# Shift and scale sums accumulated in PSUM, a third of the weight remainders made by GpSimd, and a flatter rate of requests for the first units

## Chip, cores and metric

The kernel runs on one core of a Trainium2 chip. The metric is the device time of one execution in microseconds, median of several runs. PE is TensorE, DVE is VectorE, ACT is ScalarE, POOL is GpSimd, and SP is the engine whose queue issues the DMAs.

## What is computed

One decoder layer for 256 tokens of width 4096, all in float32 (cut to what matters here):

```
mod = silu(c) @ w_ada + b_ada              # c: one vector of 4096; w_ada: 4096 x 12288
shift, scale, gate = split(mod, 3)
h = rmsnorm(x) * norm_gain
h = h * (1 + scale) + shift
proj = h @ w_in                            # 4096 x 12288
q, k, v, g_attn, u_pool, g_pool = split(proj)
y_attn = longnet_mixture(q, k, v) * silu(g_attn)       # 16 heads of 128
y_pool = multiscale_pool(u_pool, w_pool) * silu(g_pool)
y = concat(y_attn, y_pool) @ w_out         # 4096 x 4096
out = rmsnorm(x + gate * y) * final_gain
```

The weights are read once from HBM, 485 MB, and used for 256 tokens only.

## The kernel before

**Products.** A float32 weight tile is split into two parts that PE can multiply fast: ScalarE casts it (`wh`, line 237), and VectorE subtracts the cast from the original (`wl`, the remainder, line 238). The tokens are split in the same way (`hh`, `hl`). A *piece* is 2 rows of 128 of `w_in` by 512 columns, one tile `raw` of 512 KB; it makes 12 products of 128x512 (line 248): 8 that need `wh`, then 4 that need `wl`. There are 7 buffers for `raw`, and 3 each for `wh` and `wl`.

**Units.** h needs shift and scale, and these are sums over the whole of `w_ada`. The 4096 rows of h are therefore built in 16 *units* of 256 rows. For a unit 16 *tasks* are asked for (`ada_tasks`), each a `raw` tile of 512 KB of `w_ada`, on which VectorE does two steps of sum += weight * scalar (line 161, the first step of a unit line 159) into `aacc`, 128x512, in SBUF. `build_h` then has PE sum `aacc` over the partitions (line 208, four products with one column), VectorE makes the factors (lines 211 to 213), ScalarE makes h (line 221) and its cast `hh` (223), VectorE the remainder `hl` (224).

**Which work runs when.** The 24 chunks of 512 columns of `w_in` are visited in turn, as long as units are built. A *visit* (line 276) multiplies the units that are ready and that this chunk has not had yet, in one or more pieces, into one of two PSUM tiles `mm`. A chunk's first visit is copied to SBUF by ScalarE (line 289), every later one is added there by VectorE (line 291). After each piece of n rows the planner (`ada_hook`) gains n * RATES[units built] of credit, and asks for a task, at 1.456 each, while credit is above zero. A unit counts as ready two pieces after it is built. So RATES sets how soon units come, how many pieces a visit has, and how much VectorE and the DMA engines do per piece. After the 16 units the chunks get their remaining pieces, attention and pooling run in between, and the last product follows; the change does not touch that part.

Each engine runs its own queue in order. The order in it is not that of the code: the framework under the kernel lays the instructions out by its own estimate of times. PSUM has 8 banks; `mm` takes two times two, and a pool of four (`misc()`, named `psm`) serves all the rest.

Of the kernel before, what the change touches and what calls it, by code (L numbers as in the profile page):

```python
# [7 lines left out]
F32 = mybir.dt.float32  # L8
F32R = mybir.dt.float32r
AF = mybir.ActivationFunctionType  # L10
ALU = mybir.AluOpType
AX = mybir.AxisListType

P = 128
# [15 lines left out]
HB = 2  # L30
A0 = 1
WIN = 5
LAG = 2
RATES = (0.8, 0.8, 0.8, 0.5, 0.46, 0.5, 0.5, 0.5, 0.48, 0.5, 0.5, 0.54)
DEPTH = 3
HOLD = 1
EARLY = 4
# [10 lines left out]
PSB = 2  # L48
PSMB = 4
LINE = 512  # L50
RAW = PIECE * CH
ADA_COST = 0.728 * PIECE

# [2 lines left out]
def tile_hybrid_block(  # L56
# [17 lines left out]
    nc = tc.nc  # L74
# [6 lines left out]
    def slot_a(shape, dtype=F32):  # L81
        return accp.tile(shape, dtype, name="sa", bufs=16, align_bytes=LINE)

    def slot_b(shape, dtype=F32):
        return accp.tile(shape, dtype, name="sb", bufs=8, align_bytes=LINE)

# [3 lines left out]
    def misc():  # L90
        return ps_m.tile([P, CH], F32, name="psm")

    def raw_tile():
        return strm.tile([P, RAW], F32, name="raw", bufs=RAWB)

# [21 lines left out]
    adap = ada_cm.enter_context(tc.tile_pool(name="ada", bufs=2, side="right"))  # L117
# [37 lines left out]
    def ada_acc(acc, rt, kts, width, init=None):  # L155
        for i, kt in enumerate(kts):
            r = rt[:, i * width:(i + 1) * width]
            if kt == 0 and init is None:
                nc.vector.tensor_scalar(out=acc, in0=r, scalar1=cact[:, 0:1], scalar2=None, op0=ALU.mult)
            else:  # L160
                nc.vector.scalar_tensor_tensor(out=acc, in0=r, scalar=cact[:, kt:kt + 1],  # L161
                                               in1=init if kt == 0 else acc,
                                               op0=ALU.mult, op1=ALU.add)
# [3 lines left out]
    def late_work(f, lag=None):  # L167
        delayed.append(f)
        while len(delayed) > (HOLD if lag is None else lag):
            delayed.pop(0)()  # L170

    def flush_work():
        while delayed:
            delayed.pop(0)()

    def ada_tasks(u, pool):
        w = 2 * UNITS[u] * P
        n = RAW // w
        cs = slice(US[u] * P, US[u + 1] * P)
        acc = []  # L180
        tasks = []
        for a in range(0, KT, n):
            kts = list(range(a, min(KT, a + n)))

            def f(kts=kts):
                if not acc:
                    acc.append(pool.tile([P, 2 * HB * P], F32, name="aacc")[:, 0:w])
                rt = raw_tile()
                m = len(kts)
                v = rt[:, 0:m * w].rearrange("p (n s d) -> p n s d", n=m, s=2)  # L190
                if m == 1:
                    nc.sync.dma_start(out=v[:, 0], in_=wa_v[:, kts[0], 0:2, cs])
                else:
                    for i in range(2):
                        nc.sync.dma_start(out=v[:, :, i], in_=wa_v[:, kts[0]:kts[-1] + 1, i, cs])
                late_work(lambda: ada_acc(acc[0], rt, kts, w))
            tasks.append(f)
        return acc, tasks
# [4 lines left out]
    def build_h(u, acc, pool, xT):  # L203
        flush_work()
        uk, k0 = UNITS[u], US[u]
        pc = misc()
        for j in range(2 * uk):
            nc.tensor.matmul(pc[:, j:j + 1], lhsT=acc[:, j * P:(j + 1) * P], rhs=ones, start=True, stop=True)  # L208
        s12 = const.tile([P, 2, HB], F32, name="s12", bufs=2)
        ks = slice(k0, k0 + uk)  # L210
        nc.vector.tensor_tensor(out=s12[:, 0, 0:uk], in0=pc[:, 0:uk], in1=colB[:, ks], op=ALU.add)
        nc.vector.tensor_tensor(out=s12[:, 1, 0:uk], in0=pc[:, uk:2 * uk], in1=gainc[:, ks], op=ALU.mult)
        nc.vector.tensor_tensor(out=s12[:, 1, 0:uk], in0=s12[:, 1, 0:uk], in1=gb[:, ks], op=ALU.add)  # L213
        for a in range(0, uk, 2):
            kk = k0 + a
            if kk % HB == 0:
                htile[kk // HB] = [pool.tile([P, HB, S], F32R, name=n, align_bytes=LINE) for n in ("hh", "hl")]
            hh, hl = [v[:, kk % HB:kk % HB + 2] for v in htile[kk // HB]]
            hf = strm.tile([P, 2, S], F32, name="hf")
            for i in range(2):  # L220
                nc.scalar.activation(out=hf[:, i], in_=xT[:, kk + i], func=AF.Identity,  # L221
                                     scale=s12[:, 1, a + i:a + i + 1], bias=s12[:, 0, a + i:a + i + 1])
            nc.scalar.copy(out=hh, in_=hf)
            nc.vector.tensor_tensor(out=hl, in0=hf, in1=hh.bitcast(F32), op=ALU.subtract)
            for i in range(2):
                hs[kk + i] = (hh[:, i], hl[:, i])

    def split_piece(src, n, spare=False):
        rt = raw_tile()
        v = rt.rearrange("p (k n) -> p k n", n=CH)  # L230
        nc.sync.dma_start(out=v[:, 0:n], in_=src)
        if spare:
            wh, wl = [slot_a([P, PIECE, CH], F32R) for _ in range(2)]
        else:
            wh = strm.tile([P, PIECE, CH], F32R, name="wh", bufs=WHB, align_bytes=LINE)
            wl = strm.tile([P, PIECE, CH], F32R, name="wl", bufs=WLB, align_bytes=LINE)
        nc.scalar.copy(out=wh[:, 0:n], in_=v[:, 0:n])  # L237
        nc.vector.tensor_tensor(out=wl[:, 0:n], in0=v[:, 0:n], in1=wh[:, 0:n].bitcast(F32), op=ALU.subtract)  # L238
        return wh, wl

    def products(pt, hv, wh, wl, first, last):
# [102 lines left out]
    for u in range(A0):  # L344
        build_h(u, first[u][0][0], hp, xT)
# [5 lines left out]
    def ada_hook(n):  # L351
        st = state
        st["credit"] += n * RATES[min(st["built"], len(RATES) - 1)]
        st["age"] += 1
        while st["cur"] and st["cur"][1] and st["credit"] > 0:
            if len(st["cur"][1]) == 1 and min(used) < ((US[st["built"] + 1] - 1) // HB - WIN + 1) * HB:
                st["credit"] = 0.0
                break
            st["cur"][1].pop(0)()
            st["credit"] -= ADA_COST  # L360
        if st["cur"] and not st["cur"][1]:
            u = st["built"]
            build_h(u, st["cur"][0][0], hp, xT)
            st["built"] += 1
            st["age"] = 0
            st["cur"] = ada_tasks(u + 1, adap) if u + 1 < NU else None
        if st["age"] >= LAG:
            st["ready"] = st["built"]
# [3 lines left out]
    while state["ready"] < NU:  # L372
# [7 lines left out]
        else:  # L380
            ada_hook(1.0)
    hooks.remove(ada_hook)

    x_cm.close()
    ada_cm.close()
# [3 lines left out]
    def wide_tile(dtype):  # L389
        return late.tile([P, HG, S], dtype, name="tq", bufs=3, align_bytes=LINE)  # L390

# [345 lines left out]
```

## Time and profile before

| | |
|---|---|
| time, median of 3 runs | 1567.88 us (1565.35 to 1568.74) |
| the profiled execution: time, span | 1567.34 us, 1565.4 us |
| PE busy | 1516.3 us (97%), 7043 products |
| VectorE busy | 1405.4 us (90%) |
| ScalarE busy | 697.6 us (45%) |
| GpSimd busy | 0.7 us |
| chain that ended last, by engine | PE 91%, VectorE 3%, DMA 3% |
| read from HBM | 485.55 MB |

The profile is of one execution. Its views give busy time in stretches, the instructions in order of time with what ended the idle time before each, and groups of equal instructions. PE's weight loads (PEld) run beside its products and are the place where a wait of PE shows. Products are pipelined, so their own lengths overlap.

### The profile page before, as it was taken

How to read it: one execution, taken by the hardware profiler on the slowest of the kernel's cores; microseconds unless marked ns; L12 is line 12 of the kernel's file. 1: busy time of each engine (PE TensorE's matmuls, PEld its weight loads, DVE VectorE, ACT ScalarE, POOL GpSimd, SP SyncE). 2: the span in 40 equal slices, each digit the busy share in tenths (PEclk: the TensorE clock that was granted, in tenths of full speed). 3: DMA queues.
4: the chain of work that ended last, by engine and by line, in shares of the span. 5: the costliest groups of instructions: out<-in, count | busy, mean ns of one | idle time of the engine just before them, and what ended most of it. 6: DMA issues, size and time to landing. Idle time of an engine off the chain costs nothing.

```text
span 1565.4 us, 20360 instructions
## 1 busy us (share of the span) xinstructions
PE 1516.3 (97%) x7043; PEld 1257.5 (80%) x7043; DVE 1405.4 (90%) x1759; ACT 697.6 (45%) x820; POOL 0.7 (0%) x5
## 2 busy tenths in 40 slices
PE   2999999999999999999999999999999999999997
PEld 2877888888888888888888888888898888888775
DVE  5988999999999998899999998989988788898886
ACT  4655344443443434344344344556554443444433
POOL 0000000000000000000000000000000000000000
PEclk9999999999999999999999999999999999999999
DMA  9999999999999999899999998867778899998886
GB/s 331 363 335 362 321 331 321 324 308 336 327 310 327 312 330 313 294 326 326 354 340 331 330 333 307 290 226 242 231 250 273 287 357 347 318 339 324 320 305 250
DMA packets 324087, 491.11 MB, mean 314 GB/s; under 512 B 19320, under 2 KB 150664, under 8 KB 323984
## 3 DMA queue, kind: packets, MB, share of 16 engines
q1 hardware_dynamic: 323984, 489.82, 92.2%
q8 instruction: 55, 0.90, 0.2%
q14 instruction: 48, 0.39, 0.1%
HBM read 485.55 MB, written 4.19 MB: 313 GB/s over the span
## 4 chain that ended last, share of the span: by engine, by line
PE 91%; DVE 3%; DMA 3%; issue 1%; ACT 1%; SPq 0%; DVEq 0%; ACTq 0%
PE mm L248 83%; DVE aacc L161 1%; PE psm L614 1%; PE psm L248 1%; DMA raw<-in_w_ada_dram 1%; DMA raw<-in_w_in_dram 1%; PE psm L208 1%; DVE wl L238 1%; ACT wh L237 1%; PE psm L523 0%; PE psm L524 0%; PE psm L522 0%; DMA sb<-in_x_dram 0%; DMA raw<-in_w_out_dram 0%; PE psm L565 0%
## 5 line engine op out<-in xcount | busy, mean ns | idle before, releaser
L237 ACT CAST wh<-raw 128x1024 fp32r<-128x1024 f32 x514 | 538.5, 1050 | 700.0 <-PE mm L248 497.9
L238 DVE TENSOR_TENSOR wl<-raw,wh 128x1024 fp32r<-128x1024 f32 x514 | 624.5, 1218 | 45.1 <-ACT wh L237 41.9
L248 PE MATMUL mm<-wh,hh 128*128 128x512 f32 x1536 | 605.4, 394 | 4.8 <-ACT wh L237 3.8
L248 PE MATMUL mm<-wh,hl 128*128 128x512 f32 x1536 | 599.6, 390 | 0.0
L248 PE MATMUL mm<-wl,hh 128*128 128x512 f32 x1536 | 414.2, 391 | 0.6 <-DVE wl L238 0.6
L161 DVE SCALAR_TENSOR_TENSOR aacc<-raw,cact,aacc 128x512 f32<-128x512 f32 x496 | 371.0, 748 | 31.4 <-DMA raw<-in_w_ada_dram 23.8
L248 PEld LDWEIGHTS mm<-wh,hh 128*128 128x128 f32 x1536 | 288.8, 188 | 67.0 <-ACT wh L237 7.2
L248 PEld LDWEIGHTS mm<-wl,hh 128*128 128x128 f32 x1536 | 288.4, 188 | 61.1 <-DVE wl L238 1.4
L248 PEld LDWEIGHTS mm<-wh,hl 128*128 128x128 f32 x1536 | 288.9, 188 | 58.3 <-issue 0.2
L248 PE MATMUL mm<-wh,sa 128*128 128x512 f32 x896 | 224.0, 392 | 1.9 <-ACT wh L237 1.9
L248 PEld LDWEIGHTS mm<-wh,sa 128*128 128x128 f32 x896 | 167.7, 188 | 39.7 <-ACT wh L237 3.4
L161 DVE SCALAR_TENSOR_TENSOR gacc<-raw,cact,gacc 128x512 f32<-128x512 f32 x248 | 185.5, 748 | 13.5 <-DMA raw<-in_w_ada_dram 9.8
L248 PE MATMUL mm<-wl,sa 128*128 128x512 f32 x448 | 119.8, 389 | 0.0
L291 DVE TENSOR_TENSOR sa<-mm,sa 128x1024 f32<-128x1024 f32 x92 | 112.1, 1218 | 8.5 <-PE mm L248 8.4
L248 PEld LDWEIGHTS mm<-wl,sa 128*128 128x128 f32 x448 | 84.0, 188 | 17.5
L291 DVE TENSOR_TENSOR sb<-mm,sb 128x1024 f32<-128x1024 f32 x48 | 58.5, 1219 | 7.3 <-PE mm L248 7.3
L328 PE MATMUL psm<-diag_r,sb 128*128 128x128 f32 x128 | 16.9, 300 | 15.9 <-DVE diag_r L320 15.9
L221 ACT ACTIVATE hf<-xT,s 128x256 f32<-128x256 f32 x32 | 17.5, 595 | 27.9 <-DVE s L213 27.9
L328 PEld LDWEIGHTS psm<-diag_r,sb 128*128 128x128 f32 x128 | 16.6, 215 | 16.1 <-DVE diag_r L320 16.1
L289 ACT COPY sa<-mm 128x1024 f32<-128x1024 f32 x16 | 16.3, 1016 | 14.2 <-PE mm L248 14.1
L248 PE MATMUL psm<-wh,sa 128*128 128x512 f32 x80 | 20.1, 394 | 1.4 <-ACT wh L237 1.4
L248 PEld LDWEIGHTS psm<-wh,sa 128*128 128x128 f32 x80 | 14.8, 188 | 5.3 <-ACT wh L237 2.2
(113 smaller groups left out, 618.1 us busy)
## 6 DMA issues: line engine op xcount, KB each, us to landing
raw<-in_w_in_dram SPq DMA_DIRECT2D x384, 512.0 KB, 5.7
raw<-in_w_ada_dram SPq DMA_DIRECT2D x512, 256.0 KB, 5.3
raw<-in_w_ada_dram SPq DMA_DIRECT2D x128, 512.0 KB, 6.5
raw<-in_w_out_dram SPq DMA_DIRECT2D x128, 512.0 KB, 6.8
sb<-in_x_dram SPq DMA_DIRECT2D x16, 512.0 KB, 6.4
raw<-in_w_pool_dram SPq DMA_DIRECT2D x8, 512.0 KB, 4.7
out_dram<-sb SPq DMA_DIRECT2D x16, 256.0 KB, 2.6
fg<-in_final_gain_dram SPq DMA_DIRECT2D x8, 256.0 KB, 4.7
```

Of the source, the lines that this page charges most:

```text
L161: nc.vector.scalar_tensor_tensor(out=acc, in0=r, scalar=cact[:, kt:kt + 1], in1=init if kt == 0 else acc, op0=ALU.mult, op1=ALU.add)
L208: nc.tensor.matmul(pc[:, j:j + 1], lhsT=acc[:, j * P:(j + 1) * P], rhs=ones, start=True, stop=True)
L221: nc.scalar.activation(out=hf[:, i], in_=xT[:, kk + i], func=AF.Identity, scale=s12[:, 1, a + i:a + i + 1], bias=s12[:, 0, a + i:a + i + 1])
L237: nc.scalar.copy(out=wh[:, 0:n], in_=v[:, 0:n])
L238: nc.vector.tensor_tensor(out=wl[:, 0:n], in0=v[:, 0:n], in1=wh[:, 0:n].bitcast(F32), op=ALU.subtract)
L248: nc.tensor.matmul(pt[t], lhsT=hv[i][p][:, t * P:(t + 1) * P], rhs=w[:, i], start=started, stop=ended)
L289: nc.scalar.copy(out=accs[ch], in_=pt)
L291: nc.vector.tensor_tensor(out=accs[ch], in0=pt, in1=accs[ch], op=ALU.add)
L328: nc.tensor.matmul(px[:, i * S + t * P:i * S + (t + 1) * P], lhsT=xs[q][:, t, (2 * a + i) * P:(2 * a + i + 1) * P], rhs=diag_r[:, t], star ...
L614: nc.tensor.matmul(pt[t], lhsT=h[:, t * P:(t + 1) * P], rhs=w, start=False, stop=last and e == len(seq) - 1)
```

## The change

The sums of a unit grow in a bank of PSUM out of the pool of four instead of `aacc`; as PE can't read PSUM, ScalarE copies the finished 128x512 sums to SBUF (`aflat`) before the four products. While units are built, every third remainder is made by GpSimd. And RATES changes: 0.62 for the first five units in place of 0.8, 0.8, 0.5 and 0.46 (the entry in front counts for none). The diff:

```diff
-RATES = (0.8, 0.8, 0.8, 0.5, 0.46, 0.5, 0.5, 0.5, 0.48, 0.5, 0.5, 0.54)
+RATES = (0.62, 0.62, 0.62, 0.62, 0.62, 0.5, 0.5, 0.5, 0.48, 0.5, 0.5, 0.54)
+SHARE = (1, 3)
...
                 if not acc:
-                    acc.append(pool.tile([P, 2 * HB * P], F32, name="aacc")[:, 0:w])
+                    acc.append(misc()[:, 0:w])
...
     def build_h(u, acc, pool, xT):
         flush_work()
         uk, k0 = UNITS[u], US[u]
+        flat = adap.tile([P, 2 * HB * P], F32, name="aflat")
+        nc.scalar.copy(out=flat[:, 0:2 * uk * P], in_=acc)
+        acc = flat
         pc = misc()
...
+    share = {"on": True, "n": 0}
+
     def split_piece(src, n, spare=False):
...
-        nc.vector.tensor_tensor(out=wl[:, 0:n], in0=v[:, 0:n], in1=wh[:, 0:n].bitcast(F32), op=ALU.subtract)
+        eng = nc.gpsimd if share["on"] and share["n"] % SHARE[1] >= SHARE[1] - SHARE[0] else nc.vector
+        share["n"] += 1
+        eng.tensor_tensor(out=wl[:, 0:n], in0=v[:, 0:n], in1=wh[:, 0:n].bitcast(F32), op=ALU.subtract)
...
     hooks.remove(ada_hook)
+    share["on"] = False
```

The change also moves instructions in the queues. Line numbers of the new kernel are up to 8 higher (238 is 246, 291 is 299), and the number behind a name tells one buffer's use from the next.

VectorE before, where the second round of visits has begun: mm_1255 and mm_1298 are the visits that end with pieces 36 and 38, and wl_1302, wl_1325 and wl_1350 the remainders of pieces 37, 38 and 39.

```order
L238 TENSOR_TENSOR wl_1302<-raw_1299,wh_1301 128x1024
L291 TENSOR_TENSOR sa_410<-mm_1255,sa_410 128x1024
L161 SCALAR_TENSOR_TENSOR aacc_1157<-raw_1317,cact_74,aacc_1157 128x512
L238 TENSOR_TENSOR wl_1325<-raw_1322,wh_1324 128x1024
L161 SCALAR_TENSOR_TENSOR aacc_1157<-raw_1317,cact_74,aacc_1157 128x512
L161 SCALAR_TENSOR_TENSOR aacc_1157<-raw_1340,cact_74,aacc_1157 128x512 x2
L291 TENSOR_TENSOR sb_436<-mm_1298,sb_436 128x1024
L238 TENSOR_TENSOR wl_1350<-raw_1347,wh_1349 128x1024
```

In the first add here PE's next remainder (wl_1302) is already ahead of the add; at the last one it (wl_1350) stands behind.

VectorE now, at the start of the second round, which has visits of one piece: mm_1072, mm_1097 and mm_1122 are pieces 29, 30 and 31; wl_1076, wl_1126 and wl_1151 are the remainders of 29, 31 and 32. That of 30 is GpSimd's.

```order
L246 TENSOR_TENSOR wl_1076<-raw_1073,wh_1075 128x1024
L162 SCALAR_TENSOR_TENSOR psm_854<-raw_1091,cact_74,psm_854 128x512 x2
L299 TENSOR_TENSOR sa_381<-mm_1072,sa_381 128x1024
L162 SCALAR_TENSOR_TENSOR psm_854<-raw_1116,cact_74,psm_854 128x512 x2
L299 TENSOR_TENSOR sa_407<-mm_1097,sa_407 128x1024
L246 TENSOR_TENSOR wl_1126<-raw_1123,wh_1125 128x1024
L162 SCALAR_TENSOR_TENSOR psm_854<-raw_1141,cact_74,psm_854 128x512 x2
L299 TENSOR_TENSOR sb_433<-mm_1122,sb_433 128x1024
L246 TENSOR_TENSOR wl_1151<-raw_1148,wh_1150 128x1024
```

The remainders of pieces 31 and 32 stand behind the adds of pieces 30 and 31.

ScalarE before, at the first unit (xT is x transposed, hf is h before its split):

```order
L332 COPY xT<-psm 128x512 x12
L237 CAST wh<-raw 128x1024
L221 ACTIVATE hf<-xT,s_321 128x256 x2
L332 COPY xT<-psm 128x512
L223 CAST hh<-hf 128x512
```

There h comes right behind the first cast. ScalarE now, at the same place:

```order
L340 COPY xT<-psm 128x512 x12
L243 CAST wh<-raw 128x1024
L208 COPY aflat<-psm 128x512
L340 COPY xT<-psm 128x512
L225 ACTIVATE hf<-xT,s_323 128x256 x2
L340 COPY xT<-psm 128x512
L227 CAST hh<-hf 128x512
```

The new copy stands between the cast and h, and one copy of xT has moved ahead of h.

## Rows read from the trace of the kernel before

**Rows 1.** Windows: length; busy PE, PEld, DVE, ACT, POOL; PEclk, DMA share, GB/s

```profile
47.30:166.70 119.40, 114.93 (x498) 92.04 (x497) 107.24 (x129) 69.23 (x74) 0.00 (x0) 0.99 1.03 348
107.60:138.70 31.10, 30.06 (x131) 22.82 (x129) 27.59 (x37) 16.66 (x18) 0.00 (x0) 1.00 1.07 368
166.70:640.00 473.30, 473.30 (x2117) 393.01 (x2116) 446.13 (x507) 191.32 (x193) 0.00 (x0) 1.00 0.97 322
```

**Rows 2.** Timeline 937 to 941: start, length, engine, line, operation, [idle before <-releaser]

```profile
937.43 1.05 ACT L237 CAST wh<-raw 128x1024 fp32r<-128x1024 f32 x1 [1.67 <-PE mm L248]
...
937.93 1.53 DVE L161 SCALAR_TENSOR_TENSOR aacc<-raw,cact,aacc 128x512 f32<-128x512 f32 x2
...
939.38 1.22 DVE L238 TENSOR_TENSOR wl<-raw,wh 128x1024 fp32r<-128x1024 f32 x1
...
940.15 1.05 ACT L237 CAST wh<-raw 128x1024 fp32r<-128x1024 f32 x1 [1.67 <-PE mm L248]
```

**Rows 3.** Timeline of PE's weight loads: those that begin after idle time

```profile
79.58 0.19 PEld L248 LDWEIGHTS mm<-wh,hh 128*128 128x128 f32 x1 [2.47 <-ACT wh L237]
...
111.00 0.19 PEld L248 LDWEIGHTS mm<-wh,hh 128*128 128x128 f32 x1 [0.74 <-ACT wh L237]
...
131.22 0.19 PEld L248 LDWEIGHTS mm<-wh,hh 128*128 128x128 f32 x1 [0.41 <-ACT wh L237]
138.65 0.19 PEld L248 LDWEIGHTS mm<-wh,hh 128*128 128x128 f32 x1 [1.15 <-ACT wh L237]
163.16 0.76 PEld L248 LDWEIGHTS mm<-wl,hh 128*128 128x128 f32 x4 [1.06 <-DVE wl L238]
...
662.26 0.19 PEld L248 LDWEIGHTS mm<-wh,hh 128*128 128x128 f32 x1 [1.35 <-issue]
```

**Rows 4.** Windows, the ten microseconds after the first stop

```profile
80.00:90.00 10.00, 10.00 (x42) 8.11 (x40) 7.39 (x9) 4.77 (x6) 0.00 (x0) 0.83 1.07 363
```

**Rows 5.** Timeline of VectorE, 160 to 164 us

```profile
160.75 1.22 DVE L291 TENSOR_TENSOR sb<-mm,sb 128x1024 f32<-128x1024 f32 x1 [0.19 <-PE mm L248]
161.89 2.35 DVE L238 TENSOR_TENSOR wl<-raw,wh 128x1024 fp32r<-128x1024 f32 x2
```

**Rows 6.** Timeline of ScalarE, 77 to 81 us

```profile
77.58 1.01 ACT L289 COPY sb<-mm 128x1024 f32<-128x1024 f32 x1 [1.70 <-PE mm L248]
78.48 2.08 ACT L237 CAST wh<-raw 128x1024 fp32r<-128x1024 f32 x2
```

**Rows 7.** Groups of VectorE: out<-in, shapes, count | busy us, mean ns

```profile
L161 DVE SCALAR_TENSOR_TENSOR aacc<-raw,cact,aacc 128x512 f32<-128x512 f32 x496 | 371.0, 748 | 31.4 <-DMA raw<-in_w_ada_dram 23.8
...
L527 DVE SCALAR_TENSOR_TENSOR y<-psm,colA,tq 128x256 f32<-128x256 f32 x16 | 7.0, 477 | 2.1 <-PE psm L524 2.1
```

**Rows 8.** Instructions of lines 332 and 542: ns min/median/max, first and last start

```profile
L332 ACT COPY xT<-psm x16: 565/586/590, 30.7 to 47.6; 128x512 f32<-128x512 f32 x16
...
L542 POOL MEMSET bz<- x1: 526/526/526, 958.1 to 958.1; 128x512 f32 x1
```

**Rows 9.** Timeline of all engines, 28 to 48 us

```profile
28.61 14.13 DVE L161 SCALAR_TENSOR_TENSOR aacc<-raw,cact,aacc 128x512 f32<-128x512 f32 x18
...
42.16 1.05 ACT L237 CAST wh<-raw 128x1024 fp32r<-128x1024 f32 x1
...
42.89 1.02 PE L208 MATMUL psm<-ones,aacc 128*128 128x1 f32 x8 [1.25 <-DVE aacc L161]
...
43.77 3.82 PE L328 MATMUL psm<-diag_r,sb 128*128 128x128 f32 x32
...
44.47 1.09 ACT L221 ACTIVATE hf<-xT,s 128x256 f32<-128x256 f32 x2 [1.26 <-DVE s L213]
...
45.93 0.62 ACT L223 CAST hh<-hf 128x512 fp32r<-128x512 f32 x1
...
46.61 0.68 DVE L224 TENSOR_TENSOR hl<-hf,hh 128x512 fp32r<-128x512 f32 x1
...
47.66 0.39 PE L248 MATMUL mm<-wh,hl 128*128 128x512 f32 x1
```

## The prediction, made before the changed kernel ran

> **What bounds the kernel now.** First, where TensorE stands still. [rows 1] cuts the building of the units into stretches; the first column after the name is PE's busy time. From 166.7 us on PE is busy 473.30 of 473.30 us: whatever is made shorter on another engine there gains nothing. Before it, from 47.3 to 166.7, PE is busy 114.93 of 119.40.
>
> Next, what a piece takes. In [rows 2] ScalarE's cast for a new piece waits for PE each time (the engine named at the end) and starts every 2.72 us: that is PE's time for a piece of 12 products. VectorE needs 1.45 us for a pair of steps of the sums (937.93 to 939.38) and, from [rows 5], 1.14 from the start of an add to the start of a remainder.
>
> Then the stops. [rows 3] are the largest of the weight loads before which PE was idle while units were built; there are thirteen such rows, 9.98 us together. After the first one the granted clock fell to its lower level, 1.2 of 2.4 GHz, for a while: the mean of the ten microseconds from 80 is 0.83 [rows 4], which is 10 x 0.17 = 1.7 us of work less. **All that this change can win back in this phase is 11.7 us, 0.75% of the run.** By cause:
> - 2.47 us: ScalarE's copy of a finished visit stood ahead of the cast for the next piece [rows 6]. The copy waits until PE ends (1.70 idle), and the cast comes after it. 1.7 us of clock hang on it.
> - 1.17 and 1.15: the cast behind the h of a new unit (138.65 is the second).
> - 2.78 in eight rows from 111.00 to 131.22: transfers. In this stretch they moved 368 GB/s at a share of 1.07 [rows 1]. At rate 0.8 a piece of 2 k asks for 1.6/1.456 = 1.10 tasks; 2.10 tiles of 524,288 bytes in 2.72 us are 405 GB/s, more than came.
> - 1.06: a **late remainder** [rows 5]. VectorE's add of a finished visit (160.75) waits 0.19 us for PE's last product, and the remainder of PE's very next piece stands behind it. It ends at 161.89 + 1.22 = 163.11; PE's load waits until 163.16 [rows 3].
> - 1.35 at 662, behind a late weight tile of the sums.
>
> **The change part by part.** *Rates.* At 0.62 a piece asks for 1.24/1.456 = 0.85 tasks, 1.85 tiles, 357 GB/s, under the 368 that were moved. The eight transfer stops should nearly go; I keep 0.5 us. By the table the units come after pieces 14, 29, 52, 77, 100 before and 18, 39, 56, 74, 98 now; from there on the two plans run alike and end after the same 327 pieces. The total of the work is the same, but for three more adds (119 for 116), 3.4 us of VectorE, hidden.
>
> The slower start has another effect. With unit two ready only after 18 pieces, the first round is 20 visits of one piece and 4 of two, and the second round (from piece 29) has eleven visits of one piece, whose results VectorE adds. In the order before there is one remainder that stands behind the add of the piece ahead of it, that of piece 39: the stop at 163.16. **In the new order there are eight: the remainders of pieces 31, 32, 40, 52, 59, 61, 67 and 73.** The first two are in the VectorE order shown with the change, with the old place.
>
> There PE's next remainder stands twice in a row behind an add that waits for PE. Seven of the eight at 1.06 us: **+7.4**. The one of piece 40 coincides with the second unit (below). The load of VectorE there (0.85 x 1.45 + 2/3 x 1.14 + 1.14 = 3.13 us a piece against 2.72) is over PE's too, 0.41 x 11 = 4.5 us, but the stops at 31, 32 and 40 give it the time; I add nothing.
>
> *GpSimd makes every third remainder* (109 of 327). VectorE gets 1.14 us per three pieces back, and later, at rate 0.5, goes from 0.69 x 1.45 + 1.14 + 1.14/2.5 = 2.60 us a piece to 2.2. PE gains nothing by it, as it was not idle there. What GpSimd takes is in no row. Bounds: VectorE's own 1.22, and from the only GpSimd row, 526 ns for writing 512 elements [rows 8], three streams of 1024 one after the other, 3.2 us. I take two, 2.1 us, as there are two inputs. PE needs it late: the cast is done about 0.15 us after PE ends the piece three earlier (937.43 + 1.05 against PE's four remaining products of 0.23), and the remainder is wanted when two whole pieces and eight products more are done, 7.1 us later. So even 3.2 us is hidden.
>
> *Contact of GpSimd and VectorE.* Nowhere in this trace do both work. After pieces 30, 51, 60, 66 and 72 GpSimd starts on a remainder about 0.2 us after PE's end and holds until 2.3, while VectorE's late remainder would start at 0.2 + 1.14 = 1.34. They overlap for 0.96 us, five times. If one waits for the other or they take turns, that is up to 4.8 us; if they don't meet, 0; with 3.2 us for the operation, 10.3. No row is near either end; I take **+2.4**, the middle for 2.1 us.
>
> The Trainium skill has a rule that speaks against the change here: "SBUF — State Buffer", section "Who interferes with whom", says that a VectorE instruction with two SBUF inputs and a GpSimd instruction that reads SBUF exclude each other for the whole instruction. It would also leave the steps of the sums alone, as one of their inputs now lies in PSUM. "GPSIMD Engine Reference", section 3.1, has 4497 ns for 2048 elements of such an operation; the estimate from it, 2.25 us for 1024, would make five waits of 1.1, 5.5 us. No run here shows either yet.
>
> *Sums in PSUM.* Reading PSUM costs nothing: 477 ns for 256 elements from PSUM (L527) and 748 for 512 from SBUF (L161) [rows 7] lie on one line of 1.06 ns an element. Writing it is in no row; I take the same time, with 0.1 us a step to either side. That counts at the start alone, where 18 steps in a row take 14.13 us [rows 9]: up to 1.8 either way.
>
> *The copy back to SBUF*, 128x512 by ScalarE: 0.59 us [rows 8], 16 times, on the way from the last step to PE's four small products. At the start (the ScalarE order shown with the change) it stands behind the first cast, and one copy of the transposed x has come ahead of h. By [rows 9]: cast until 43.2, copy until 43.8, small products until 44.9, first quarter of the transposes (3.82/4) until 45.9, copy 46.5, hf 47.6, copy 48.1, hh 48.7, hl 49.3, when the second product can run; before it ran at 47.6. **+1.7.** Later units: most have their last step more than a piece ahead of PE's products. Not the second: step behind the add of piece 38, products waiting 0.4, then h ahead of the cast for 41 and the remainder of 40 behind the add of 39, **+1.6** in all. Nor the third and fourth, where the last pair of steps ends about when PE does: copy and two signals, **+0.75 and +0.85**. The first unit +0.2: its cast now stands ahead of h.
>
> **The sum:** 1.7 + 0.2 + 7.4 + 1.6 + 1.6 + 0.5 + 2.4 = 15.4 us lost, where 11.7 were lost before: +3.7. The profiled execution took 1567.34 (span 1565.4), within 0.6 of the median 1567.88; its sum is 1571.0. On the median, **1571.6**, 0.24% more. About 0.2%, 3.1 us, is what a measurement of this kernel can tell from no change.
>
> **The rivals.**
> - *Contact in full.* One waits for the other all the 0.96 us, five times: 4.8 us (10.3 with the longer operation) in place of 2.4, 1574.0 to 1579.5, say 1575. A stop of over 2 us can bring the lower clock again, as after 79.58; each costs 1.7. (This is what the page on SBUF of the Trainium skill would give.)
> - *Late remainders at half price.* The price is one event's. If most adds find PE already late for another reason, 3.7 go, and without contact 2.4 more: 1565.5 to 1568, say 1567, no change. For it: PE also stops for the units there. Against: add and remainder follow PE's end whatever came before.
> - *Relief wins (faster).* If PE's end of a visit comes later than the remainder behind its add is needed in hardly any of the eight places, or VectorE runs so far ahead that they don't bind, 9 us and the contact fall away, and some of the 0.75 and 0.85 too: 1558 to 1560. It decides if fewer than about three of the eight stops appear. For it: the 11.7 us are real, and causes one to three do go.
> - *It does not do what it says:* GpSimd starts late or steps in PSUM are a little slower, all hidden: 1568 to 1570.
>
> **How the numbers follow.** Forecast 0.38 (contact 0 to 4: 1569.2 to 1573.2), contact in full 0.27, half price 0.16, relief 0.15, nothing 0.04. Slower by over 0.2% is above 1571.0: 0.6 of the forecast and all of the contact, 0.50. Faster, below 1564.8: 0.15. Between: 0.35. The range, 1563.5 to 1579.5, leaves out most of the relief and the clock's fall on top of full contact, under 0.2 together.
>
> **What would show it.** Eight stops of about a microsecond with VectorE's remainder as their end, between 130 and 265 us, none of them later; no 2.47 us stop and no lower clock near 80; PE's first wide product near 49; GpSimd's rows near 2.1 us; VectorE's remainders longer than 1.22, or idle before them, only where GpSimd runs. It is wrong if those stops are absent, or if PE stops after 265 us, which would mean that GpSimd's remainders arrive too late.

## The result and the profile after

The changed kernel takes **1583.78 us** (median of 6 runs, 1579.92 to 1589.07), the kernel before 1568.31 in the same sessions (6 runs, 1565.35 to 1569.11): ratio 1.0097, 95% interval 1.0082 to 1.0112, **15.5 us slower**. The forecast was 1571.6 with a range up to 1579.5: the sign was right, the size was not, and the time lies outside the range.

The page of the kernel after: its span, and the groups of the instructions that the change touches (busy time, mean ns of one, then idle time ahead of them). They answer to [rows 7].

```profile
span 1583.1 us, 20397 instructions
L246 DVE TENSOR_TENSOR wl<-raw,wh 128x1024 fp32r<-128x1024 f32 x405 | 517.8, 1283 | 74.7 <-ACT wh L243 69.7
L162 DVE SCALAR_TENSOR_TENSOR psm<-raw,cact,psm 128x512 f32<-128x512 f32 x496 | 372.8, 752 | 18.9 <-DMA raw<-in_w_ada_dram 9.6
L246 POOL TENSOR_TENSOR wl<-raw,wh 128x1024 fp32r<-128x1024 f32 x109 | 268.1, 2459 | 701.2 <-ACT wh L243 680.6
```

A step into PSUM takes 752 ns against 748: nothing changed there. A remainder takes GpSimd 2459 ns, twice VectorE's time, and VectorE's own remainders have become longer, 1283 on average against 1218.

Where TensorE lost it (the stretches of [rows 1], same columns):

```profile
47.30:166.70 119.40, 116.36 (x510) 93.60 (x510) 95.11 (x113) 70.10 (x76) 32.01 (x14) 0.99 0.96 319
166.70:640.00 473.30, 464.21 (x2045) 380.80 (x2044) 409.65 (x451) 188.54 (x195) 138.55 (x56) 0.99 0.96 320
```

Up to 166.7 PE is now a little busier than before (116.36 for 114.93), so the transfer stops did go. After it, where PE had been busy without a gap (473.30), 9.1 us are missing. VectorE has less to do in both stretches: the loss isn't its load on average.

The weight loads before which PE was idle (answering to [rows 3]; the number in brackets is the idle time, the name is what ended it):

```profile
106.93 0.77 PEld L256 LDWEIGHTS mm<-wl,hh 128*128 128x128 f32 x4 [0.79 <-POOL wl L246]
135.66 0.77 PEld L256 LDWEIGHTS mm<-wl,hh 128*128 128x128 f32 x4 [1.05 <-DVE wl L246]
163.81 1.16 PEld L256 LDWEIGHTS mm<-wl,hh 128*128 128x128 f32 x4 [1.34 <-DVE wl L246]
201.70 0.77 PEld L256 LDWEIGHTS mm<-wl,hh 128*128 128x128 f32 x4 [1.03 <-DVE wl L246]
224.00 0.77 PEld L256 LDWEIGHTS mm<-wl,hh 128*128 128x128 f32 x4 [2.43 <-DVE wl L246]
253.19 0.76 PEld L256 LDWEIGHTS mm<-wl,hh 128*128 128x128 f32 x4 [1.35 <-DVE wl L246]
354.14 0.76 PEld L256 LDWEIGHTS mm<-wl,hh 128*128 128x128 f32 x4 [2.43 <-DVE wl L246]
924.05 0.76 PEld L256 LDWEIGHTS mm<-wl,hh 128*128 128x128 f32 x4 [2.46 <-DVE wl L246]
```

There are 24 such stops before the products of pieces now, 23.54 us, for 13 with 9.98 before; one more, 0.47 us at 272.39, stands before a unit's four small products and waits for ScalarE's copy out of PSUM. The 24 divide so: six late remainders (pieces 31, 32, 52, 61, 67, 73) 6.78; four stops of 1.35 to 2.46 at pieces 59, 68, 103 and 308, 8.66; the second unit (163.81 to 169.76, four rows) 3.24; GpSimd's remainder late (six rows between 97 and 198) 3.05; ScalarE's cast 1.16; two small ones 0.64.

Two of these kinds in their own rows. First a late remainder, on VectorE, as in [rows 5]: the add waits for PE, the remainder follows, and it ends at 135.61, when PE's load of 135.66 can go.

```profile
133.25 1.23 DVE L299 TENSOR_TENSOR sa<-mm,sa 128x1024 f32<-128x1024 f32 x1 [0.34 <-PE mm L256]
134.39 1.22 DVE L246 TENSOR_TENSOR wl<-raw,wh 128x1024 fp32r<-128x1024 f32 x1
```

Second the stop at 224.00: VectorE and GpSimd in the same microseconds.

```profile
220.22 1.22 DVE L299 TENSOR_TENSOR sa<-mm,sa 128x1024 f32<-128x1024 f32 x1 [0.61 <-PE mm L256]
221.36 2.58 DVE L246 TENSOR_TENSOR wl<-raw,wh 128x1024 fp32r<-128x1024 f32 x1
220.49 2.37 POOL L246 TENSOR_TENSOR wl<-raw,wh 128x1024 fp32r<-128x1024 f32 x1 [6.58 <-ACT wh L243]
```

VectorE's remainder takes 2.58 us where 1.22 is the rule. GpSimd's ends at 222.86, VectorE's at 223.94, 1.08 later: it waited until GpSimd was through and then ran in full. Of VectorE's 405 remainders 18 take more than 1.5 us, and in every one the end is 1.08 or 1.09 us after that of GpSimd's, however long they overlapped. The remainder of h (`hl`), which also has two inputs in SBUF, meets GpSimd too: here it takes 2.90 us where 0.69 is the rule.

```profile
343.93 2.90 POOL L246 TENSOR_TENSOR wl<-raw,wh 128x1024 fp32r<-128x1024 f32 x1 [6.14 <-ACT wh L243]
344.48 2.90 DVE L228 TENSOR_TENSOR hl<-hf,hh 128x512 fp32r<-128x512 f32 x1
```

Seven microseconds later VectorE, so put back, meets GpSimd again, and PE stops for 2.43 at 354.14 (piece 103). Contact also lengthened the stop of piece 32 (1.55 in place of 1.05) and made the last row of the second unit (1.19 at 169.76; its remainder took 3.20) and the two small ones. Less the 1.06 of a late remainder at piece 59, that is 9.9 us of stops by contact.

After the stop of 224.00 the granted clock fell to its lower level, as in [rows 4], and so it did after the stops of 354.14 and 924.05 and around the second unit (160 to 170): the mean is 0.83 in each of these four stretches of ten microseconds, 1.7 us of work less. The first of them (columns as above, the granted clock is the third number from the end):

```profile
220.00:230.00 10.00, 8.00 (x28) 6.10 (x27) 7.83 (x8) 2.51 (x3) 2.37 (x1) 0.83 0.67 218
```

The account: stops 23.54 - 9.98 = 13.6; lower clock (4 - 1) x 1.7 = 5.1; first wide product at 48.66 for 47.34, 1.3. Together 20.0; the first piece after the 327 of this phase begins 18.5 us later than before (979.30 for 960.82). The account is a little over, as weight loads stand idle before the products do.

### The profile page after: what moved, and what is told of

Same layout as the page of the kernel before. It is cut to its first block, busy times and chain, and to the rows that moved or that the text cites. A ratio compares the mean times of both kernels' runs of the same rounds, so it can differ in the third digit from the quotient of the medians.

```text
span 1583.1 us, 20397 instructions
## 1 busy us (share of the span) xinstructions
PE 1525.5 (96%) x7043; PEld 1260.8 (80%) x7043; DVE 1333.6 (84%) x1653; ACT 705.7 (45%) x836; POOL 268.8 (17%) x114
## 4 chain that ended last, share of the span: by engine, by line
PE 87%; DVE 6%; DMA 4%; issue 2%; ACT 1%; SPq 0%; POOL 0%; DVEq 0%; ACTq 0%
PE mm L256 78%; DVE wl L246 2%; DVE psm L162 2%; PE psm L256 2%; DMA raw<-in_w_ada_dram 2%; DMA raw<-in_w_in_dram 1%; PE psm L623 1%; PE psm L212 1%; DMA sb<-in_x_dram 1%; PE psm L574 0%; PE psm L444 0%; PE psm L461 0%; PE psm L533 0%; PE psm L420 0%; SPq L196 0%
## 5 line engine op out<-in xcount | busy, mean ns | idle before, releaser
L246 DVE TENSOR_TENSOR wl<-raw,wh 128x1024 fp32r<-128x1024 f32 x405 | 517.8, 1283 | 74.7 <-ACT wh L243 69.7
L256 PE MATMUL mm<-wl,hh 128*128 128x512 f32 x1536 | 416.0, 392 | 13.6 <-DVE wl L246 12.9
L162 DVE SCALAR_TENSOR_TENSOR psm<-raw,cact,psm 128x512 f32<-128x512 f32 x496 | 372.8, 752 | 18.9 <-DMA raw<-in_w_ada_dram 9.6
L246 POOL TENSOR_TENSOR wl<-raw,wh 128x1024 fp32r<-128x1024 f32 x109 | 268.1, 2459 | 701.2 <-ACT wh L243 680.6
L299 DVE TENSOR_TENSOR sa<-mm,sa 128x1024 f32<-128x1024 f32 x95 | 116.0, 1221 | 45.1 <-PE mm L256 44.4
```

The lines of the kernel that those rows point to most:

```text
L246: eng.tensor_tensor(out=wl[:, 0:n], in0=v[:, 0:n], in1=wh[:, 0:n].bitcast(F32), op=ALU.subtract)
L256: nc.tensor.matmul(pt[t], lhsT=hv[i][p][:, t * P:(t + 1) * P], rhs=w[:, i], start=started, stop=ended)
L299: nc.vector.tensor_tensor(out=accs[ch], in0=pt, in1=accs[ch], op=ALU.add)
```

## The experiments

Two theories stood after the result. **Contact:** VectorE's and GpSimd's remainders wait for each other, and this makes the large stops. **Load:** the rates put steps of the sums into the round of single pieces, where VectorE has too much to do. The forecasts of the first four runs name three: A, the rates make the loss; B, GpSimd's share makes it; C, the sums in PSUM do. Medians with their ratio to the kernel before; 1568 us is that kernel in each session. Every edit makes the framework lay out the queues anew, so no difference between two of these kernels is that of one part alone; rows are read from one execution of each.

| kernel | us | ratio, 95% interval |
|---|---|---|
| new rates alone | 1576.55 | 1.0057 (1.0041 to 1.0073) |
| all but the new rates | 1568.84 | 1.0009 (0.9990 to 1.0028) |
| all but GpSimd's share | 1592.43 | 1.0165 (1.0126 to 1.0203) |
| all but the sums in PSUM | 1634.77 | 1.0422 (1.0406 to 1.0438) |
| all, GpSimd not reading | 1568.43 | 1.0009 (0.9998 to 1.0020) |
| GpSimd's share alone | 1620.67 | 1.0337 (1.0319 to 1.0355) |
| sums in PSUM alone | 1568.97 | 1.0005 (0.9990 to 1.0019) |
| all but the new rates, first unit in SBUF | 1564.36 | 0.9984 (0.9972 to 0.9997) |
| all, other rates | 1564.16 | 0.9979 (0.9968 to 0.9990) |
| the same, first unit in SBUF | 1560.81 | 0.9961 (0.9946 to 0.9977) |
| before, other rates | 1557.86 | 0.9941 (0.9928 to 0.9953) |

**New rates alone.** The kernel before with the new RATES:

```diff
-RATES = (0.8, 0.8, 0.8, 0.5, 0.46, 0.5, 0.5, 0.5, 0.48, 0.5, 0.5, 0.54)
+RATES = (0.62, 0.62, 0.62, 0.62, 0.62, 0.5, 0.5, 0.5, 0.48, 0.5, 0.5, 0.54)
```

> Only the new RATES; all remainders on VectorE, sums in SBUF. The order has nine remainders behind the add of the piece ahead (pieces 31, 32, 35, 37, 39, 48, 54, 59, 73), no late cast. Theory A (the rates make the late remainders, 0.93 us each in the changed kernel; GpSimd's contact raises some of them to 2.3 and those let the clock fall for another 1.6): without GpSimd each costs 0.9 to 1.0, 8.5 us, in place of some 9 of the 10 us lost before: 1566 to 1571 us, no stop over 1.6 us, no lower clock between 60 and 950 us. Theory B (GpSimd's share costs, whatever the rates): 1560 to 1564. Theory C (sums in PSUM cost): 1560 to 1564.

1576.55: above the forecast of 1566 to 1571, more than the late remainders that were priced. The timeline of VectorE in this kernel, and PE's waits beside it:

```profile
153.28 0.75 DVE L162 SCALAR_TENSOR_TENSOR aacc<-raw,cact,aacc 128x512 f32<-128x512 f32 x1
153.94 1.23 DVE L243 TENSOR_TENSOR wl<-raw,wh 128x1024 fp32r<-128x1024 f32 x1
155.08 0.76 DVE L162 SCALAR_TENSOR_TENSOR aacc<-raw,cact,aacc 128x512 f32<-128x512 f32 x1
155.74 1.23 DVE L296 TENSOR_TENSOR sa<-mm,sa 128x1024 f32<-128x1024 f32 x1
156.87 0.75 DVE L162 SCALAR_TENSOR_TENSOR aacc<-raw,cact,aacc 128x512 f32<-128x512 f32 x1
157.53 1.23 DVE L296 TENSOR_TENSOR sa<-mm,sa 128x1024 f32<-128x1024 f32 x1
155.22 1.21 PE L253 MATMUL mm<-wl,hh 128*128 128x512 f32 x4 [0.50 <-DVE wl L243]
157.11 0.47 PE L253 MATMUL mm<-wh,hh 128*128 128x512 f32 x1 [0.68 <-DVE sa L296]
```

VectorE works without a gap from 144 to 160. PE waits for remainders, and at 157.11 for an add, since a new visit needs the PSUM tile that the add empties. Here an add no longer waits for PE: VectorE is behind. PE's queue has in this stretch the products of two pieces interleaved. The 24 products from 149.9 took 7.18 us and the 24 from 157.1 took 7.61, the second unit among them, where two pieces take 5.44 (the 7.2 and 7.6 that a forecast below gives to single pieces are those of pairs). So in the round of single pieces the load counts.

**All but the new rates:** the changed kernel with the RATES of before.

> GpSimd's third and the sums in PSUM with the old RATES. The order has no remainder behind the add of the piece ahead, one late cast (piece 12). Theory A: the late cast with its clock (about 4 us) and the units stay as before, the start costs 1.3 more, a few contacts of 0.5 to 2.3 us remain: 1565 to 1574, and few stops after 200 us. Theory B: GpSimd's cost stays, 1578 to 1586. Theory C: 1578 to 1586.

1568.84, no change against before. GpSimd's share and the sums in PSUM together are neutral at the old rates, though 13 of VectorE's remainders take more than 1.5 us there as well (up to 3.36 us). Ten of them stop PE nowhere, as VectorE is ahead of it; the three of 152.55, 193.39 and 227.88 make stops of 0.87, 0.47 and 0.96 us. GpSimd's remainder is late six times, 2.96 us. All the stops together are 9.99 us, as before.

**All but GpSimd's share:** every remainder on VectorE again.

```diff
-    share = {"on": True, "n": 0}
+    share = {"on": False, "n": 0}
```

> The new RATES and sums in PSUM, all remainders on VectorE. Eight remainders behind the add of the piece ahead (31, 32, 35, 37, 39, 48, 59, 73). Theory A: eight times about 0.95, 1.3 at the start, no contact, no fall of the clock by it: 1566 to 1572. Theory B: 1562 to 1567. Theory C: 1578 to 1586.

1592.43, 8.6 us above the changed kernel and above all three forecasts: GpSimd's share is a gain at these rates, not the cost. It is also 16 us above the new rates alone. The profiled executions of the two lie further apart, 1602.07 and 1574.34, and their rows show where. The first wide product comes 4.6 us later (51.72 for 47.09, see the start below). Stops before the products of pieces make 31.8 us (39 rows) for 23.3. Five more, 7.15 us, stand before the small products of a unit, for one of 1.25:

```profile
231.21 1.05 ACT L243 CAST wh<-raw 128x1024 fp32r<-128x1024 f32 x1 [2.46 <-DMA raw<-in_w_in_dram]
232.16 0.58 ACT L208 COPY aflat<-psm 128x512 f32<-128x512 f32 x1
232.79 0.97 PEld L212 LDWEIGHTS psm<-ones,aflat 128*128 128x128 f32 x8 [1.96 <-ACT aflat L208]
298.39 0.97 PEld L212 LDWEIGHTS psm<-ones,aflat 128*128 128x128 f32 x8 [2.32 <-ACT aflat L208]
366.77 0.97 PEld L212 LDWEIGHTS psm<-ones,aflat 128*128 128x128 f32 x8 [2.27 <-ACT aflat L208]
```

ScalarE's copy out of PSUM takes 0.58 us, but at these three places it stands behind a cast that waits for a transfer (2.46, 2.54 and 1.65 us), and PE behind the copy. The clock fell after them, and at 170: the means of 170 to 180, 235 to 245, 300 to 310 and 365 to 375 us are 0.83, 0.66, 0.66 and 0.83, 10.2 us of work less, where the new rates alone have no such fall after the first wide product. So at these rates the copy back is not free. How much of the difference is the copy's and how much the new order's was not tested.

**All but the sums in PSUM:** the sums in SBUF, no copy back.

```diff
-                    acc.append(misc()[:, 0:w])
+                    acc.append(pool.tile([P, 2 * HB * P], F32, name="aacc")[:, 0:w])
```

> The new RATES and GpSimd's third, sums in SBUF. Ten remainders behind the add of the piece ahead (31, 32, 34, 40, 46, 52, 58, 61, 67, 73). The steps of the sums now also have two SBUF inputs. Theory A with contact for every VectorE instruction of that form (the Trainium skill, SBUF — State Buffer, section Who interferes with whom): more instructions stretched, VectorE's steps too, some up to 2 to 3 us: 1585 to 1605. Theory A with contact for remainders alone: 1580 to 1590. Theory B: as the changed kernel, 1580 to 1588. Theory C: 1566 to 1570.

1634.77, 51 us above the changed kernel and 30 above the highest forecast. The same two groups in it:

```profile
L162 DVE SCALAR_TENSOR_TENSOR aacc<-raw,cact,aacc 128x512 f32<-128x512 f32 x496 | 494.2, 996 | 17.4 <-DMA raw<-in_w_ada_dram 8.2
L243 POOL TENSOR_TENSOR wl<-raw,wh 128x1024 fp32r<-128x1024 f32 x109 | 300.1, 2753 | 720.3 <-ACT wh L240 702.1
```

A step with both inputs in SBUF now takes 996 ns on average; next to the same GpSimd work a step with its sum in PSUM took 752. By instruction it is plainer: here the 117 steps that overlap a remainder of GpSimd take 1800 ns on average and the other 379 take 748, while in the changed kernel the 177 that overlap one take 752, the longest 757. So steps of that form meet GpSimd too, and the sums in PSUM are what makes its share bearable.

**GpSimd's share alone:** the kernel before with that part only.

> The kernel before with GpSimd's third of the remainders alone: old rates, sums of shift and scale in SBUF. Theory A (a VectorE step whose two inputs both lie in SBUF waits for a GpSimd remainder as a whole, and a step that reads its sum from PSUM doesn't; without sums in PSUM nearly every GpSimd remainder meets such a step): steps at 900 us or more per thousand (mean over 900 ns against 748), GpSimd's mean over 2.6 us, and at the old rates about half of the early steps per piece that the changed rates ask for, so half of the 51 us that the changed kernel lost when its sums went back to SBUF: 1580 to 1600. Rival B (at the old rates VectorE has room enough beside GpSimd, as it had with sums in PSUM, 1568.8): 1565 to 1572.

1620.67: the mechanism as expected (steps 1008 ns, GpSimd 2690), the cost higher than the 1580 to 1600 forecast. That the old rates ask for fewer early steps doesn't halve it: the steps of all sixteen units meet GpSimd, up to the end of the phase at 960 us.

**Sums in PSUM alone.**

> The kernel before with the sums of shift and scale in PSUM alone: old rates, all remainders on VectorE. Theory A (a step into PSUM costs what a step in SBUF does, 752 against 748 ns, and only the start loses, by the copy before the first unit and the lower clock behind it): first wide product at 48.5 to 51.1 us instead of 47.3, time 1569 to 1573. Rival B (a unit's copy out of PSUM on ScalarE and the buffer that the sums keep make stops at every unit): 1575 or more.

1568.97, no difference that can be measured, though the start is later than forecast (52.04, below). In the profiled execution one unit's copy out of PSUM also comes late: PE waits 2.85 us for it at 721.75, and the clock falls behind that (0.83 from 720 to 730). Rival B had expected such stops at every unit.

**All, GpSimd not reading.** GpSimd waits for the cast as before, then writes zeros instead of subtracting (a third of the remainders is left out):

```diff
+        if eng is nc.gpsimd:
+            eng.tensor_tensor(out=wl[:, 0:n, 0:4], in0=v[:, 0:n, 0:4], in1=wh[:, 0:n, 0:4].bitcast(F32),
+                              op=ALU.subtract)
+            for _ in range(2):
+                eng.memset(wl[:, 0:n].bitcast(F32), 0.0)
+            return wh, wl
```

> The changed kernel, but where GpSimd has a remainder it only reads eight elements a partition (so that it still waits for the cast) and then writes zeros over the tile twice: it is busy about as long, but reads nothing from SBUF meanwhile. It leaves out a third of the remainders of the unit-building phase. Theory A (contact: VectorE's remainder, with two inputs in SBUF, and GpSimd's wait for each other as whole instructions): in the changed kernel's trace the stretched VectorE remainders (2.58, 3.77, 3.34 us against 1.22) made four stops of 1.35 to 2.46 us; less the 0.93 of a late remainder at one of them they lost 2.30 - 0.93 + 1.22 + 2.29 + 2.32 = 7.2 us, and the lower clock after three of them 3 x 1.6 = 4.8. So 1583.8 - 12 = 1572, between 1569 and 1575; no VectorE remainder over 1.5 us, no stop over 1.6 us after the first 60 us, late remainders at eight pieces still there at about 1 us each. Rival B (the stops come from the load that the early steps put on VectorE, not from two engines reading at once): 1581 to 1585, with stops over 2 us still there.

1568.43: **the whole loss is gone**, all 15.4 us, a little more than the 12 forecast (the range began at 1569; the 3.77 us that the forecast names is two remainders, 2.63 and 1.22). VectorE and GpSimd again at the same time, and the granted clock around it:

```profile
222.55 0.20 POOL L247 TENSOR_TENSOR wl<-raw,wh 128x8 fp32r<-128x8 f32 x1 [7.36 <-ACT wh L243]
222.82 1.96 POOL L250 MEMSET wl<- 128x1024 f32 x2
223.58 1.21 DVE L252 TENSOR_TENSOR wl<-raw,wh 128x1024 fp32r<-128x1024 f32 x1
220.00:230.00 10.00, 9.37 (x42) 7.44 (x41) 9.51 (x12) 4.51 (x5) 2.11 (x3) 1.00 0.74 236
```

GpSimd is busy from 222.55 to 224.78, and the remainder that begins inside takes its usual 1.21. None of VectorE's remainders is stretched. Stops: 12.2 us for 23.54, and none behind a remainder is longer than 1.34. One of 1.70 at 169.23, behind a cast at the second unit, is longer than the forecast allowed (1.6), and the clock fell there (0.66 from 165 to 175). Late remainders stay (pieces 31, 40, 52, 59, 61, 73 in its rows), at 1.03 to 1.34 each. Its order isn't quite that of the changed kernel (pieces 34 and 37 are late in place of 32 and 67), and its start is 2.9 us later, so the contact is worth about 15 to 18 us, and not a figure to the tenth. The rows of the changed kernel give the same: 9.9 us of stops and three falls of the clock at 1.7, 15.0.

**The start.** In the kernels with the copy out of PSUM, PE's wait ahead of the first unit's small products is 2.11 to 2.37 us, where [rows 9] have 1.25. In order: the changed kernel, then the changed kernel with the old rates; the wait, and the granted clock from 44 to 48 us:

```profile
42.55 1.05 PE L212 MATMUL psm<-ones,aflat 128*128 128x1 f32 x8 [2.37 <-ACT aflat L208]
44.00:48.00 4.00, 4.00 (x24) 4.00 (x23) 2.19 (x5) 2.73 (x6) 0.00 (x0) 0.57 1.06 369
43.36 1.71 PE L212 MATMUL psm<-ones,aflat 128*128 128x1 f32 x8 [2.11 <-ACT aflat L208]
44.00:48.00 4.00, 4.00 (x20) 4.00 (x20) 0.82 (x5) 0.98 (x2) 0.00 (x0) 0.50 1.09 367
```

At the lower clock the 32 transposes that follow take 5.45 and 6.41 us where they took 3.82, and the first wide product comes at 48.66 and 51.10. To take it away, the first unit's sums stay in SBUF and the rest stays in PSUM (old rates; one of its two places is shown, the other leaves out the copy back for that unit):

```diff
-                    acc.append(misc()[:, 0:w])
+                    acc.append((misc() if u >= A0 else pool.tile([P, CH], F32, name="aacc", bufs=1))[:, 0:w])
```

> The changed kernel with the old rates and with the first unit's sums in SBUF; GpSimd has its third and the sums of the later units grow in PSUM. Theory A (the copy out of PSUM before the first unit and the lower clock behind it cost 1 to 4 us in the kernel with the old rates): first wide product at 47.3 to 47.6 us, 1564 to 1567, all runs within 4 us of each other, where the kernel with the old rates spread over 1564.3 to 1574.3. Rival B (that spread comes from elsewhere): 1566 to 1570 and a spread of over 6 us.

1564.36, 4.5 below the same kernel with the copy, which ran in another session. The first wide product is at 47.51, the wait and the clock are these:

```profile
43.05 1.02 PE L213 MATMUL psm<-ones,aacc 128*128 128x1 f32 x8 [0.85 <-DVE aacc L162]
44.00:48.00 4.00, 4.00 (x35) 3.98 (x35) 3.30 (x7) 3.26 (x7) 0.00 (x0) 1.00 1.07 368
```

The spread shrank from 10 to 6.6 us, not to the 4 expected, so a part of it has another source.

**Other rates.** The changed kernel with rates whose order has no remainder behind an add and no cast behind a copy:

```diff
-RATES = (0.62, 0.62, 0.62, 0.62, 0.62, 0.5, 0.5, 0.5, 0.48, 0.5, 0.5, 0.54)
+RATES = (0.8, 0.77, 0.7, 0.5, 0.5, 0.5, 0.5, 0.5, 0.48, 0.5, 0.5, 0.54)
```

> The changed kernel with other rates: (0.8, 0.77, 0.7, 0.5, 0.5, then as before) in place of five times 0.62. In its order no piece has its remainder behind a sum or its cast behind a copy; GpSimd's share and the sums in PSUM are as changed. Theory A (the loss of the change is that the rates put steps into the round of single pieces, where remainders queue behind sums; GpSimd and PSUM are neutral): with neither late remainders nor the late cast of the kernel before (2.47 us in its trace), 1568.8 of the old rates with GpSimd and PSUM, less 2.5, = 1566, between 1562 and 1569; ratio to before 0.996 to 1.000. Rival B (any shift of steps towards the single pieces costs): 1573 or more. Rival C (GpSimd's slower remainders make new stops wherever the casts are late): 1570 to 1576, with over ten stops put down to GpSimd.

1564.16, as forecast: 19.6 us faster than the change, with 15 stretched remainders (up to 3.21 us) still in it. Nine stops, 4.5 us, are GpSimd's. With the first unit in SBUF as well:

> As the kernel with other rates, but the first unit's sums stay in SBUF as in the kernel before, so that TensorE needs no copy out of PSUM before the first unit; the later units' sums grow in PSUM. Theory A (the copy adds 1.1 us to TensorE's wait ahead of the first unit, 2.37 against 1.25 in the two traces, and after the longer wait the granted clock of the next stretch is 0.50 to 0.93 instead of 1.00, so that 32 transposes take 5.45 or 6.41 us instead of 3.82): the first wide product at 47.3 to 47.6 us in every profile instead of 48.7 to 51.1, and the time 1 to 4 us below the kernel with other rates, with a smaller spread: 1561 to 1565. Rival B (the start is hidden behind the transfers of the first pieces): no difference within 1 us.

1560.81: 3.4 less, just under the forecast, first wide product at 47.60 for 48.81. In these two executions that isn't the clock, which stayed at 1.00 behind the longer wait too.

**Before, other rates.** Nothing but the new numbers in the kernel before:

> The kernel before with these other rates alone: all remainders on VectorE, sums in SBUF. In its order one remainder is late, at piece 42, and no cast is; the kernel before has one late remainder and one late cast. Theory A (rates count by the late places that they make): the late cast goes (2.47 us in the trace of before), VectorE is fuller in the single-piece round than with GpSimd's help, so 1565 to 1569. Rival B (without GpSimd's share VectorE falls behind in the single-piece round as it did with the changed rates alone, where pieces 37 and 38 took 7.2 and 7.6 us): 1570 or more.

**1557.86, the fastest of all, 10.2 us below before, and below both forecasts.** In its whole unit phase only these stops are left:

```profile
91.82 0.19 PEld L248 LDWEIGHTS mm<-wh,hh 128*128 128x128 f32 x1 [1.16 <-ACT wh L237]
125.25 0.19 PEld L248 LDWEIGHTS mm<-wh,hh 128*128 128x128 f32 x1 [0.89 <-ACT wh L237]
130.86 0.19 PEld L248 LDWEIGHTS mm<-wh,hh 128*128 128x128 f32 x1 [0.26 <-ACT wh L237]
164.45 0.76 PEld L248 LDWEIGHTS mm<-wl,hh 128*128 128x128 f32 x4 [1.06 <-DVE wl L238]
```

3.37 us for 9.98; no fall of the clock (1.7); the first wide product at 46.34 for 47.34. That is 9.3 of the 9.8 us between the two spans. The forecast had missed that the transfer stops would go with the late cast.

## Why the prediction was wrong in size

*Contact in full* was the rival that came true, but with a price three times mine. The step that failed is the price of contact, 2.4 us in the sum; about 15 came in its place. A second one failed beside it: GpSimd's remainder was to be hidden, and made 3.05 us of stops.

- **Contact, the term that failed.** I took 2.4 us, and 4.8 if they wait for each other in full, from five places with 0.96 us each. The runs show about 15: 9.9 in stops and 5.1 by the clock. The length was wrong: the stretched remainder of 221.36 is 1.36 us longer than 1.22, that of 920.66 (3.34 us) 2.12, since nothing fixes how much of GpSimd's remainder is left. The places were wrong too: I had GpSimd start 0.2 us after PE's end, as if the cast were never late, and looked for contact only at late remainders. At none of the five did they meet: GpSimd started 0.4 to 2.6 us after VectorE's late remainder had ended. Of the four large stops, that of piece 59 was on my list of late remainders without contact, and those of pieces 68, 103 and 308 were on no list. The remainder of h I left out altogether. And I left the fall of the clock to a clause: three of the four stops brought it, 1.7 us each. My sign of being wrong, stops after 265 us, came (354.14, 924.05), but not for the reason that I gave: VectorE's stretched remainders made them, not late ones of GpSimd.
- **The rule that the prediction cited.** One engine waits until the other is done (VectorE's end is GpSimd's plus 1.08), and a step with one input in PSUM is spared (752 ns against 996). This agrees with the rule of the Trainium skill, "SBUF — State Buffer", section "Who interferes with whom", by which whole instructions exclude each other. It spoke against this change, and weighing it at half was the mistake.
- **GpSimd's remainder, 2.1 us.** Its median is 2.40, close to the estimate of 2.25 worked out from the Trainium skill, "GPSIMD Engine Reference", section 3.1. "Even 3.2 us is hidden" failed: six stops, 3.05 us, between 97 and 198, where casts came late. I had read the cast's lead from rows near 937 us. In the first round it stands behind ScalarE's copy of a finished visit or the h of a unit (the first four stops: the cast of 93.42, for the stop at 97.00, follows a copy that waited for PE); at the last two (189.79 and 198.06) it waited for a transfer.
- **Late remainders, 7 x 1.06.** Right: the rows have 1.03 to 1.06 at five of the six plain ones, and the places were those that the order names; piece 32 (1.55) and piece 59, the seventh, met GpSimd.
- **VectorE's load, "I add nothing".** In the changed kernel nothing speaks against it: with a GpSimd that doesn't read, the time is 1568.43, no slower than before. But that hangs on GpSimd's share. With all remainders on VectorE it fell behind in the round of single pieces (1576.55 with the new rates alone). "PE gains nothing by it", of GpSimd's share, holds at the old rates only (1568.84 with it, 1568.97 without): at the new rates 1592.43 without the share stands against 1568.43 with one that doesn't read, a relief of 24 us, of which the contact took 15 back.
- **Sums in PSUM.** Right for the step (752 for 748), though not by the line that I drew: two points always lie on one. The start, 1.7, was 1.3 in the profiled execution, near it by luck: I had only the copy in the queue, and the lower clock behind the longer wait adds 1.6 to the transposes (5.45 for 3.82). In other kernels with the copy it was 1.5 to 4.7 us. Of the third and fourth units, 0.75 and 0.85, only the fourth has a stop in the rows, 0.47 at 272.39; the second cost 3.24 in stops instead of 1.6, 1.19 of it by contact, and a fall of the clock.
- **The sum without contact.** It was 1569.2 (1571.6 less 2.4), and the kernel whose GpSimd doesn't read took 1568.43. That is closer than the terms deserve: in its profiled execution the start was 4.2 us late in place of 1.7.
- **What the change wins.** Right: the stop of 2.47 us at 79.58 with its clock and the transfer stops are gone.

Open: of the 16 us by which the sums in PSUM at the new rates, without GpSimd, are worse than the rates alone, the rows show the late start, the copies behind late casts and the clock; no run parts them.

## What to carry to other kernels

Before a second engine gets a share of elementwise work, list which of the first engine's instructions read the same memory with two inputs: those wait for its whole instruction, and it matters where the first engine has no lead over TensorE. A table that spaces side work was worth more here than new helpers: the same number of steps, moved so that 3.37 us of stops are left of 9.98, gave 10 us with no other change. And price a long stop of TensorE (2.4 us here) with the clock that it may cost behind it.

## What the runs showed of the hardware

- VectorE's and GpSimd's remainders (two inputs in SBUF each) exclude each other in both directions: in the changed kernel VectorE's went from 1.22 to as much as 3.34 us, GpSimd's from 2.40 to 3.44. VectorE's ended 1.08 or 1.09 us after GpSimd's each time. GpSimd writing zeros (2 us) stretched none. A step whose sum lies in PSUM isn't stretched beside GpSimd either (177 of them, the longest 757 ns).
- VectorE's first step of a sum, one input from SBUF, takes 747 ns into PSUM and 481 into SBUF; the further steps take the same into either (752, 748).
- At the start PE's waits of 2.11 to 2.37 us were followed by the lower granted clock in five of six profiles (the two shown: 0.57 and 0.50 from 44 to 48 us), those of 0.85 to 1.82 us by none; once, in the changed kernel with other rates, the clock stayed at 1.00 behind a wait of 2.11. Later the length of a stop alone doesn't tell: in the changed kernel all three of 2.43 to 2.46 us brought the lower clock, and so did the second unit, whose longest was 1.34, while in the kernel with all but the sums in PSUM those of 3.29 (144.42) and 3.37 (195.25) brought none.
